# A hybrid attention layer on one core: low parts of the weights kept in DRAM, and half of the attention's transfers issued by GpSimd

## The chip, the cores and the metric

The kernel runs on one core of a Trainium2 chip. The metric is the time of one execution on the device in microseconds, measured over whole executions; the profile is one execution of its own, and its span goes from the first instruction to the last.

The core's engines run side by side, each through its own list of instructions, in order: TensorE (PE in the profile; PEld its weight loads), VectorE (DVE), ScalarE (ACT), GpSimd (POOL) and SyncE (SP), which here only issues transfers. An instruction waits for semaphores; while it waits, everything behind it on its engine waits too.

## The reference

One decoder layer over 2048 tokens of width 1024 in fp32. A single projection feeds three mixers: A, attention over the 256 best keys of an indexer; B, differential attention of two softmax maps; C, three dilated windows. Then the output projection, a norm, a gated feed-forward block and a second norm:

```python
def reference(x, w_in, w_o, lam, subln_g, ln1_g, ln1_b, w_gate, w_up, w_down, ln2_g, ln2_b):
    for l in range(DEPTH):
        lambda_init = 0.8 - 0.6 * math.exp(-0.3 * l)
        mix = hybrid_mixer(x, w_in[l], w_o[l], lam[l], subln_g[l], lambda_init)
        x = layer_norm(DEEPNORM_ALPHA * x + mix, ln1_g[l], ln1_b[l])
        f = (jax.nn.silu(x @ w_gate[l]) * (x @ w_up[l])) @ w_down[l]
        x = layer_norm(DEEPNORM_ALPHA * x + f, ln2_g[l], ln2_b[l])
    return x
```

## The kernel before

**Three products for one.** Every fp32 operand of the large products is split: its high part is the value rounded to the fp32r type, its low part is value minus high part, also fp32r. A product is then three matmuls: high by high, high by low, low by high (`mm3`, L1224 to L1230: L1227, L1228 and L1229 are these three; the low part of the weights enters in L1229).

**The order in time.** Until about 1169 us the kernel projects the input, ranks the keys for A and runs C together with A and B of the first 512 tokens. From there on two programs are woven together (`weave`, L751): the *trunk*, which takes the tokens in four groups g = 0 to 3 of 512, and the *attention* A and B of groups 1 to 3, which runs ahead of the trunk. For each group the trunk has a `head` (L1242: transpose the mixed rows, output projection `wo`, norm, transpose again) and a `body` (L1319: gate `fg`, up `fu` and down `fd` products in six stages `HV` of 4 or 3 chunks of 128 hidden columns). A planner in `weave` hands out the two programs by estimated costs, and a scheduler beneath it sets the final order of each engine's list at build time; at run time the lists are fixed.

**The weights' stream.** A `Stream` (L484) brings the weights of the trunk as tiles: w_o, gate and up tiles of 128x1024, down tiles of 128x512 or 128x384. `read` loads a raw tile (`fr` in the profile, two buffers), `divide` splits it by `split` (L149): ACT rounds the high part (L151), then POOL subtracts for the low part (L152; DVE instead for the tiles numbered 0, 2 and 4 of each stage, `HURRY`), both into one tile `f` with two buffers. `take` splits one tile ahead of the one that PE works on and reads two more. Each group streams and splits all weights anew. A raw buffer is free again when both the rounding and the subtraction are done, so the next load into it waits for POOL or DVE.

**The transfers.** `load` and `store` (L143 to L147) are both issued by SP: the raw weights, all loads of A and B (keys `ak`, `bk`, queries `aq`, `bq`, values `va`, `vb`, selection `se`), their results to DRAM (`mixd<-oa`, `mixd<-ob`), the mixed rows for the heads (`mx`, L1235: 128x1024 in two buffers `mx`), the residual rows `r` and the output. POOL issues only the joined results of C. On SP and on POOL alike a transfer may also wait for the one issued eight before it on the same engine, since each engine has eight semaphores for them.

Of the kernel before, what the change touches and what calls it, by code (L numbers as in the profile page):

```python
# [21 lines left out]
P = 128  # L22
# [28 lines left out]
F_RAWS = 2  # L51
NORMS = (0, 2)
# [6 lines left out]
RL = 3  # L59
MX_BUFS = 2  # L60
# [31 lines left out]
def tile_hybrid_layer(  # L92
# [391 lines left out]
    class Stream:  # L484
# [3 lines left out]
        def __init__(self, pool_, specs, raws, bufs, name, hurried=()):  # L488
            self.pool, self.specs, self.raws, self.bufs, self.name = pool_, specs, raws, bufs, name
            self.raw, self.tiles, self.pos, self.hurried = [], [], 0, hurried  # L490

        def read(self, upto):
            while len(self.raw) < min(upto, len(self.specs)):
                src = self.specs[len(self.raw)]
                n = src.shape[1]
                t = self.pool.tile([P, 1024], F32, name=f"{self.name}r{len(self.raw)}", tag="raw", bufs=self.raws)[:, :n]
                load(t, src)
                self.raw.append((t, n))

        def divide(self, upto):  # L500
            while len(self.tiles) < min(upto, len(self.specs)):
                i = len(self.tiles)
                self.read(i + 1)
                r, n = self.raw[i]
# [32 lines left out]
    def project(pt, w_, tl):  # L537
        wv = w_.rearrange("p a (k n) -> p a k n", k=KC)
        for k in range(KC):
            PE.matmul(pt, wv[:, 0, k], tl[0][:, k], start=(k == 0), stop=False)  # L540
            PE.matmul(pt, wv[:, 0, k], tl[1][:, k], start=False, stop=False)  # L541
            PE.matmul(pt, wv[:, 1, k], tl[0][:, k], start=False, stop=(k == KC - 1))  # L542
# [37 lines left out]
    def natural(kns, n, tl, name, tiles):  # L580
# [196 lines left out]
    def a_block(tp, g, qb, tab, ak, va):  # L777
# [6 lines left out]
        for r in (0, 64):  # L784
            load(q[r:r + 64].rearrange("p a h t -> p (a h) t").bitcast(F32), qad.rearrange("a (h r) t -> r (a h) t", r=64)[:, :, cols])
        if qb >= 2:
            se = tp.tile([P, wg_], BF16, name=f"se{qb}", tag="se")
            load(se[:, :w], seld[qb][:, :w])
# [29 lines left out]
        store(mixd[cols, 0:256], oa)  # L818
# [46 lines left out]
    def b_head(tp, g, h, tab):  # L865
# [6 lines left out]
        for m in range(2):  # L872
            k = tp.tile([P, wg_], F32R, name=f"bk{h}{m}_{g}", tag="bk", bufs=BK_BUFS[g])
            for r in range(0, P, 32):
                load(k[r:r + 32].bitcast(F32), kbd[r // 32 % 2, (2 * h + m) * 32:(2 * h + m + 1) * 32, 0:wg_])
            ks.append(k)
        for r in range(0, P, 32):
            load(q[r:r + 32].bitcast(F32), qbd[r // 64, h * 64:h * 64 + 64].rearrange("(m r) t -> r m t", m=2)[:, :, cols])
        vb = tp.tile([P, 4 * g + 4, P], F32R, name=f"vb{h}_{g}", tag="vb")
        load(vb.bitcast(F32), vbd[h].rearrange("(b p) d -> p b d", p=P)[:, 0:4 * g + 4, :])  # L880
# [36 lines left out]
        store(mixd.rearrange("(b p) d -> p b d", p=P)[:, 4 * g:4 * g + 4, 256 + h * 64:320 + h * 64], ob)  # L917

    def attention(g):
# [25 lines left out]
        load(ak.bitcast(F32), kad[:, 0:wg_])  # L945
        va = tp.tile([P, 4 * g + 4, P], F32R, name=f"va{g}")
        load(va.bitcast(F32), vad.rearrange("(b p) d -> p b d", p=P)[:, 0:4 * g + 4])
# [264 lines left out]
    f_specs, hurried = [], set()  # L1212
    for g in range(4):
        if g < 3:
            f_specs += [w_o[dc] for dc in range(8)]
        for f0, nf in HV:
            hurried.update(len(f_specs) + i for i in HURRY)
            for f in range(f0, f0 + nf):
                f_specs += ([w_gate[f]] if f > f0 or not f0 or g < EARLY else []) + [w_up[f]]
# [300 lines left out]
```

## Time and profile before

| | us |
|---|---|
| median of 3 runs | 3438.15 (3437.69 to 3444.48) |
| the profiled execution | 3439.7 |
| its span | 3437.9 |
| PE busy in the span | 3140.8 (91%) |
| POOL busy | 985.1 (29%) |
| DMA, mean over the span | 434.76 MB, 126 GB/s |

The table's lower part is from the profile's first part and from its line on DMA. A busy PE is not PE at its peak, because the ends of matmuls are modelled; what is sure is where PE stood still, and at what granted clock it ran. Those two are read from the waits and from tables of stretches.

### The profile page before, as it was taken

The page shows a single profiled execution, that of the slowest core. Times are in us where ns is not written, and L with a number is a line of the kernel's source. Part 1 is how long each engine was busy: PE and PEld are TensorE (multiplying, and loading weights), DVE is VectorE, ACT ScalarE, POOL GpSimd, SP SyncE. Part 2 cuts the span into 40 slices and gives each one's busy share as a digit, 9 for nine tenths or more (in the row PEclk, how much of TensorE's full clock was granted, in tenths as well). Part 3 has the DMA queues.
Part 4 walks back from the last instruction along what each step waited for, and adds up shares of the span by engine and source line. Part 5 has one row for each costly group of instructions (what it writes and reads, how often), then busy time and mean ns, then how long its engine had stood idle before and what let it go on. Part 6 is the DMA issues. An engine that isn't in the chain of part 4 may idle for free.

```text
span 3437.9 us, 45436 instructions
## 1 busy us (share of the span) xinstructions
PE 3140.8 (91%) x15994; PEld 2596.8 (76%) x15994; DVE 2076.5 (60%) x5353; ACT 1648.1 (48%) x2767; POOL 985.1 (29%) x587
## 2 busy tenths in 40 slices
PE   8898889858978799989998999999899999999997
PEld 7776667758878678877876788777678788778885
DVE  4879699546788576645458655465855555352224
ACT  3756646436756355545443545354454444232222
POOL 3221323014232222232223223321423232343332
PEclk9999999979999799999999999999999999999999
DMA  7464655588776633242245332423434232333322
GB/s 219 159 182 134 198 169 175 168 185 201 183 149 150 192 93 107 83 116 71 67 120 156 93 105 85 128 63 82 138 97 118 79 117 71 137 103 95 98 87 85
DMA packets 261206, 434.76 MB, mean 126 GB/s; under 512 B 49648, under 2 KB 149488, under 8 KB 256624
## 3 DMA queue, kind: packets, MB, share of 16 engines
q1 hardware_dynamic: 257776, 427.65, 43.8%
q0 software_dynamic: 1120, 3.67, 0.5%
q8 instruction: 126, 2.06, 0.3%
q14 instruction: 104, 0.85, 0.1%
q10 hardware_dynamic: 2080, 0.52, 0.1%
HBM read 331.65 MB, written 100.11 MB: 126 GB/s over the span
## 4 chain that ended last, share of the span: by engine, by line
PE 53%; DVE 6%; DMA 3%; issue 2%; ACT 2%; POOL 1%; SPq 0%; DVEq 0%; ACTq 0%; POOLq 0%
PE fg L1229 4%; PE fu L1229 4%; PE fu L1227 4%; PE fg L1227 4%; PE fu L1228 4%; PE fg L1228 4%; PE fd L1229 4%; PE fd L1227 4%; PE fd L1228 4%; PE wo L1227 1%; PE wo L1229 1%; PE wo L1228 1%; PE a_0o L854 1%; PE a_2o L854 1%; PE a_0t L845 1%
## 5 line engine op out<-in xcount | busy, mean ns | idle before, releaser
L152 POOL TENSOR_TENSOR f<-fr,f 128x1024 fp32r<-128x1024 f32 (+2 forms) x320 | 567.9, 1776 | 1438.5 <-ACT f L151 1389.9
L151 ACT CAST f<-fr 128x1024 fp32r<-128x1024 f32 (+2 forms) x392 | 321.4, 820 | 499.6 <-PE fd L1229 168.8
L1229 PE MATMUL fd<-h,f 128*128 128x512 f32 x704 | 282.1, 401 | 9.9 <-POOL f L152 9.9
L1227 PE MATMUL fd<-h,f 128*128 128x512 f32 x704 | 284.7, 405 | 4.1 <-ACT f L151 4.1
L1227 PE MATMUL fg<-xt,f 128*128 128x512 f32 x704 | 281.8, 400 | 0.8 <-DVE b_13m L895 0.3
L1227 PE MATMUL fu<-xt,f 128*128 128x512 f32 x704 | 281.2, 399 | 1.5 <-ACT f L151 1.5
L1229 PE MATMUL fg<-xt,f 128*128 128x512 f32 x704 | 278.8, 396 | 4.0 <-DVE f L152 2.9
L1228 PE MATMUL fd<-h,f 128*128 128x512 f32 x704 | 281.4, 400 | 0.0
L1229 PE MATMUL fu<-xt,f 128*128 128x512 f32 x704 | 278.4, 395 | 2.2 <-DVE f L152 1.2
L1228 PE MATMUL fg<-xt,f 128*128 128x512 f32 x704 | 278.2, 395 | 0.0
L1228 PE MATMUL fu<-xt,f 128*128 128x512 f32 x704 | 277.6, 394 | 0.0
L540 PE MATMUL pj<-xt,w 128*128 128x512 f32 x544 | 219.0, 403 | 26.6 <-DVE st L563 9.9
L542 PE MATMUL pj<-xt,w 128*128 128x512 f32 x544 | 216.7, 399 | 1.4 <-POOL w L152 1.4
L541 PE MATMUL pj<-xt,w 128*128 128x512 f32 x544 | 216.8, 399 | 0.7 <-POOL xt L152 0.7
L1355 DVE TENSOR_TENSOR fu<-sg,fu 128x512 f32<-128x512 f32 x88 | 61.1, 694 | 247.1 <-PE fu L1229 205.2
L1023 ACT ACTIVATE c<-c,ob 128x256 f32<-128x256 f32 (+1 forms) x384 | 156.5, 457 | 102.6 <-DVE ob L1017 101.7
L1371 DVE TENSOR_TENSOR rT<-rT,fd 128x512 f32<-128x512 f32 x160 | 109.4, 685 | 145.7 <-PE fd L1229 144.8
L1229 PEld LDWEIGHTS fd<-h,f 128*128 128x128 f32 x704 | 134.9, 192 | 42.3 <-POOL f L152 15.9
L152 POOL TENSOR_TENSOR w<-wr,w 128x1024 fp32r<-128x1024 f32 (+2 forms) x42 | 99.7, 2378 | 221.8 <-ACT w L151 186.3
L1227 PEld LDWEIGHTS fd<-h,f 128*128 128x128 f32 x704 | 134.9, 192 | 31.9 <-ACT f L151 6.8
L1229 PEld LDWEIGHTS fg<-xt,f 128*128 128x128 f32 x704 | 132.6, 188 | 32.8 <-DVE f L152 4.0
L1229 PEld LDWEIGHTS fu<-xt,f 128*128 128x128 f32 x704 | 132.5, 188 | 31.7 <-DVE f L152 3.0
(813 smaller groups left out, 8061.2 us busy)
## 6 DMA issues: line engine op xcount, KB each, us to landing
fr<-in_w_gate_dram SPq DMA_DIRECT2D x88, 512.0 KB
fr<-in_w_up_dram SPq DMA_DIRECT2D x88, 512.0 KB
fr<-in_w_down_dram SPq DMA_DIRECT2D x128, 256.0 KB
wr<-in_w_in_dram SPq DMA_DIRECT2D x42, 512.0 KB
fr<-in_w_o_dram SPq DMA_DIRECT2D x24, 512.0 KB
fr<-in_w_down_dram SPq DMA_DIRECT2D x64, 192.0 KB
ocd<-ob SPq DMA_DIRECT2D x16, 528.0 KB
ot<-ocd SPq DMA_DIRECT2D x32, 264.0 KB
```

The lines of the kernel that those rows point to most:

```text
L151: A.copy(hi, src)
L152: lo_eng.tensor_tensor(lo, src, hi.bitcast(F32), op=ALU.subtract)
L540: PE.matmul(pt, wv[:, 0, k], tl[0][:, k], start=(k == 0), stop=False)
L541: PE.matmul(pt, wv[:, 0, k], tl[1][:, k], start=False, stop=False)
L542: PE.matmul(pt, wv[:, 1, k], tl[0][:, k], start=False, stop=(k == KC - 1))
L854: PE.matmul(acc[:, :m], vfun(b), pt[:, i, c0:c0 + m], start=(b == 0 and i == 0), stop=(b == n - 1 and i == 1))
L1023: A.activation(nl, nl, AF.Exp, bias=ob[:, place(blk), 65:66], scale=-1.0)
L1227: PE.matmul(pt, wv[:, 0, k], hi[:, k], start=(k == 0), stop=False)
L1228: PE.matmul(pt, wv[:, 0, k], lo[:, k], start=False, stop=False)
L1229: PE.matmul(pt, wv[:, 1, k], hi[:, k], start=False, stop=(k == n - 1))
L1355: V.tensor_tensor(pt, sg, pt, op=ALU.mult)
L1371: V.tensor_tensor(d, d, pt, op=ALU.add)
```

## The change

**Low parts kept.** `Stream` gets a list of DRAM tensors, one for each weight tile (`lowd`). High and low part become two tiles, `f` with two buffers and `fl` with three. The first group still subtracts, and stores each low part to DRAM (100 stores, 37 MiB). In groups 1 to 3 SP loads the low parts (292 loads, 107 MiB), and their subtractions are gone: 238 on POOL and 54 on DVE. The stream of the last head's w_o (`g`) and that of the projection split as before.

**Transfers by POOL.** `fetch` issues from POOL where g is 2 or 3, from SP otherwise. By it go all loads and stores of A and B, the mixed rows and the residual rows: 172 transfers move from SP to POOL. The attention of group 2 begins while the trunk is still in group 0.

**Mixed rows in halves.** `read_mix` loads 128x512 into the four buffers `sg` that the gate's results use, in place of two buffers of its own.

```diff
+    def fetch(g, dst, src):
+        (G if g > 1 and OWN_QUEUE else SY).dma_start(out=dst, in_=src)
...
-        def __init__(self, pool_, specs, raws, bufs, name, hurried=()):
+        def __init__(self, pool_, specs, raws, bufs, name, hurried=(), kept=None, ahead=0):
...
                 load(t, src)
                 self.raw.append((t, n))
+                j = i - self.raws
+                if 0 <= j < len(self.tiles) and self.kept[j] is not None and id(self.kept[j]) not in self.stored:
+                    self.stored.add(id(self.kept[j]))
+                    store(self.kept[j], self.tiles[j][1][:, :self.raw[j][1]].bitcast(F32))
+
+        def low(self, upto):
+            while len(self.lows) < min(upto, len(self.specs)):
+                i = len(self.lows)
+                t = self.pool.tile([P, 1024], F32R, name=f"{self.name}l{i}", tag="wl", bufs=self.bufs + self.ahead)
+                there = self.kept[i] is not None and id(self.kept[i]) in self.stored
+                if there:
+                    load(t[:, :self.specs[i].shape[1]].bitcast(F32), self.kept[i])
+                self.lows.append((t, there))
...
-                t = self.pool.tile([P, 2, 1024], F32R, name=f"{self.name}{i}", tag="w", bufs=self.bufs)
-                split(t[:, 0, :n], t[:, 1, :n], r, V if i in self.hurried else G)
-                self.tiles.append(t)
+                hi = self.pool.tile([P, 1024], F32R, name=f"{self.name}{i}", tag="w", bufs=self.bufs)
+                lo, there = self.lows[i]
+                A.copy(hi[:, :n], r)
+                if not there:
+                    (V if i in self.hurried else G).tensor_tensor(lo[:, :n], r, hi[:, :n].bitcast(F32), op=ALU.subtract)
+                self.tiles.append((hi, lo))
...
             self.divide(i + min(n + 2, self.bufs))
+            self.low(i + self.bufs + self.ahead)
             self.read(len(self.tiles) + self.raws)
...
             for r in range(0, P, 32):
-                load(k[r:r + 32].bitcast(F32), kbd[r // 32 % 2, (2 * h + m) * 32:(2 * h + m + 1) * 32, 0:wg_])
+                fetch(g, k[r:r + 32].bitcast(F32), kbd[r // 32 % 2, (2 * h + m) * 32:(2 * h + m + 1) * 32, 0:wg_])
...
-    def read_mix(hp, g, t):
-        mx = hp.tile([P, D], F32, name=f"mx{g}{t}", tag="mx", bufs=MX_BUFS)
-        load(mx, mixd[rows(g, t), :])
+    def read_mix(hp, g, i):
+        mx = hp.tile([P, 512], F32, name=f"mx{g}{i}", tag="sg", bufs=RL)
+        fetch(g, mx, mixd[rows(g, i // 2), i % 2 * 512:i % 2 * 512 + 512])
...
-    fs = Stream(fp, f_specs, F_RAWS, F_BUFS, "f", hurried)
+    fs = Stream(fp, f_specs, F_RAWS, F_BUFS, "f", hurried, [lowd[key] for key in f_keys], 1)
```

**Where instructions stand now.** The scheduler orders all engines anew, so that small shifts are found everywhere. At three places the lists differ in kind. In them L152 is `fetch` in the changed kernel, L144 and L147 are `load` and `store`, L532 is the subtraction.

SP's list in the body of group 1. Before, raw tiles and the attention's loads alternate:

```order
L144 DMA fr_20030<-in_w_gate_dram 128x1024
L144 DMA fr_20069<-in_w_up_dram 128x1024
L144 DMA bq_2_20289<-qbd 32x2x512 x3
L144 DMA bk_2_21187<-kbd 32x1536
L144 DMA fr_20134<-in_w_down_dram 128x512
L144 DMA bk_2_21187<-kbd 32x1536 x3
```

After, nothing but a low part and a raw tile in turn:

```order
L144 DMA fl_20302<-lowu_13507 128x1024
L144 DMA fr_20304<-in_w_gate_dram 128x1024
L144 DMA fl_20355<-lowg_13508 128x1024
L144 DMA fr_20357<-in_w_up_dram 128x1024
L144 DMA fl_20399<-lowu_13509 128x1024
L144 DMA fr_20401<-in_w_gate_dram 128x1024
```

The attention's loads have left SP here, and each low part stands one place ahead of a raw tile.

POOL's list in group 0, stage 16 (down tiles of 128x384, numbered dc 0 to 7), where B of group 2 begins. Before, POOL makes the table of distances and then only low parts:

```order
L152 TENSOR_TENSOR f_18258<-fr_18132,f_18258 128x384
L773 IOTA tab_18360 128x1536
L775 AFFINE_SELECT tab_18360<-tab_18360 128x128
L152 TENSOR_TENSOR f_18326<-fr_18197,f_18326 128x384
L152 TENSOR_TENSOR f_18346<-fr_18261,f_18346 128x384
L152 TENSOR_TENSOR f_18391<-fr_18329,f_18391 128x384
```

After, the results of A's last two blocks and the first head's loads stand between them:

```order
L532 TENSOR_TENSOR fl_18500<-fr_18434,f_18563 128x384
L800 IOTA tab_18671 128x1536
L152 DMA bk_2_18677<-kbd 32x1536
L152 DMA mixd<-oa_17760 128x256
L532 TENSOR_TENSOR fl_18566<-fr_18501,f_18633 128x384
L152 DMA mixd<-oa_17774 128x256
L532 TENSOR_TENSOR fl_18636<-fr_18567,f_18655 128x384
L802 AFFINE_SELECT tab_18671<-tab_18671 128x128
L152 DMA bk_2_18677<-kbd 32x1536 x3
L152 DMA bk_2_18682<-kbd 32x1536 x4
L152 DMA bq_2_18676<-qbd 32x2x512 x4
L152 DMA vb_2_18691<-vbd 128x12x128
```

Twelve transfers in a row stand behind the low part of dc 2 (`fl_18636`) and ahead of that of dc 3. On PE the head's first logits, which stood behind all of dc 3 and dc 4, now stand behind their first two matmuls alone.

The start of A of group 3, in the body of group 1. Before, on SP, the loads stand between raw tiles:

```order
L147 DMA mixd<-ob_2_21203 128x4x64
L144 DMA fr_22053<-in_w_up_dram 128x1024
L144 DMA ak_22073<-kad 128x2048
L144 DMA va_22075<-vad 128x16x128
L144 DMA aq_22077<-qad 64x8x128 x2
L144 DMA se_22080<-sel_102 128x1664
L144 DMA aq_22088<-qad 64x8x128 x2
L144 DMA fr_22116<-in_w_down_dram 128x512
```

After, on POOL, which has no low parts to make here:

```order
L152 DMA mixd<-ob_2_21602 128x4x64
L152 DMA ak_22493<-kad 128x2048
L152 DMA va_22495<-vad 128x16x128
L152 DMA aq_22497<-qad 64x8x128 x2
L152 DMA se_22500<-sel_102 128x1664
L800 IOTA bi_22502 128x1664
L152 DMA aq_22508<-qad 64x8x128
L802 AFFINE_SELECT bi_22502<-bi_22502 128x128
```

The loads follow the last result of group 2's B at once, with no raw tile between.

## Rows read from the trace of the kernel before

**Rows 1.** The page's first part: busy time, share of the span, instructions.

```profile
span 3437.9 us, 45436 instructions
...
PE 3140.8 (91%) x15994; PEld 2596.8 (76%) x15994; DVE 2076.5 (60%) x5353; ACT 1648.1 (48%) x2767; POOL 985.1 (29%) x587
```

**Rows 2.** Table of stretches: ends, length, busy us by engine, granted clock, DMA share, GB/s.

```profile
1273.70:1803.80 530.10, 511.40 (x2535) 413.44 (x2535) 290.13 (x727) 264.55 (x392) 142.62 (x88) 0.97 0.32 92
...
1900.40:2426.20 525.80, 508.95 (x2519) 409.64 (x2518) 286.41 (x678) 249.39 (x344) 150.03 (x88) 0.99 0.34 96
```

**Rows 3.** PE's waits, 1803.8 to 3100 us: line, waited for, us in total, times, longest.

```profile
PE fd L1229 <- POOL f L152: 6.9, 4, 2.3
...
PE mt L1264 <- DMA mx<-mixd: 5.0, 3, 2.8
PE b_0l L826 <- DMA bq<-qbd: 4.9, 1, 4.9
...
PE a_0l L826 <- DMA aq<-qad: 2.6, 1, 2.6
...
PE a_0l L826 <- DVE a_0m L828: 2.2, 1, 2.2
```

**Rows 4.** Table of further stretches, columns as in rows 2.

```profile
790.00:1130.00 340.00, 288.44 (x2258) 272.93 (x2257) 265.88 (x1232) 212.06 (x515) 116.94 (x117) 0.93 0.73 164
...
1719.00:1741.00 22.00, 15.72 (x48) 10.40 (x47) 6.99 (x17) 5.30 (x8) 5.34 (x6) 0.78 0.80 198
...
2180.00:2210.00 30.00, 25.25 (x99) 19.43 (x98) 12.43 (x39) 8.67 (x11) 12.62 (x6) 0.89 0.58 149
2404.00:2414.00 10.00, 5.87 (x12) 3.34 (x12) 4.71 (x14) 2.69 (x4) 1.97 (x2) 0.66 0.73 185
...
2680.00:2710.00 30.00, 25.44 (x104) 20.17 (x103) 16.28 (x32) 9.08 (x12) 11.96 (x6) 0.89 0.30 97
```

**Rows 5.** SP's waits over the span, columns as in rows 3.

```profile
SPq L144 <- POOL f L152: 1268.8, 302, 23.4
```

**Rows 6.** Groups of instructions: shapes, count, busy us, mean ns, idle before, releasers.

```profile
L1371 DVE TENSOR_TENSOR rT<-rT,fd 128x512 f32<-128x512 f32 x160 | 109.4, 685 | 145.7 <-PE fd L1229 144.8
...
L152 POOL TENSOR_TENSOR f<-fr,f 128x1024 fp32r<-128x1024 f32 (+2 forms) x320 | 567.9, 1776 | 1438.5 <-ACT f L151 1389.9 <-PE b_1l L826 24.4 <-PE wo L1229 7.1
```

**Rows 7.** Tile mixd: transfers by line and issuer, ns of an issue (min/median/max); POOL's landing.

```profile
L147 SPq DMA_DIRECT2D mixd<-oa x16: 326/336/432, 767.8 to 2393.3; - x16
...
L1111 POOL DMA_DIRECT2D mixd<-ot x14: 926/927/1062, 802.3 to 1127.5; - x14
...
DMA to landing us min/median/max: 3.2/6.6/10.7
```

**Rows 8.** SP in order of time: start us, us, line, transfer, count.

```profile
1719.83 2.75 SPq L144 DMA_DIRECT2D bk<-kbd  x6
1722.69 2.12 SPq L144 DMA_DIRECT2D bq<-qbd  x4
```

**Rows 9.** POOL in order of time, the low part of dc 3.

```profile
1720.02 1.02 POOL L152 TENSOR_TENSOR f<-fr,f 128x384 fp32r<-128x384 f32 x1 [0.59 <-ACT f L151]
```

**Rows 10.** PE in order of time; in brackets idle before and releaser.

```profile
1724.95 0.40 PE L1228 MATMUL fd<-h,f 128*128 128x512 f32 x1
...
1725.88 0.39 PE L1229 MATMUL fd<-h,f 128*128 128x512 f32 x1
1730.37 0.73 PE L826 MATMUL b_0l<-bk,bq 128*128 128x512 f32 x2 [4.10 <-DMA bq<-qbd]
```

**Rows 11.** SP in order of time, where A of group 3 begins.

```profile
2172.79 5.14 SPq L144 DMA_DIRECT2D aq<-qad  x2
```

**Rows 12.** SP in order of time, where B of group 3 begins.

```profile
2396.98 3.24 SPq L144 DMA_DIRECT2D bq<-qbd  x4
```

**Rows 13.** SP in order of time, a raw tile of 128x384 in group 3.

```profile
3360.23 0.33 SPq L144 DMA_DIRECT2D fr<-in_w_down_dram  x1
```

**Rows 14.** ACT in order of time, the rounding of that tile.

```profile
3362.71 0.52 ACT L151 CAST f<-fr 128x384 fp32r<-128x384 f32 x1 [1.95 <-DMA fr<-in_w_down_dram]
```

More of the change, by code (lines that the diff above doesn't have):

```diff
@@ L484, in tile_hybrid_layer @@
     class Stream:
-        def __init__(self, pool_, specs, raws, bufs, name, hurried=()):
+        def __init__(self, pool_, specs, raws, bufs, name, hurried=(), kept=None, ahead=0):
             self.pool, self.specs, self.raws, self.bufs, self.name = pool_, specs, raws, bufs, name
-            self.raw, self.tiles, self.pos, self.hurried = [], [], 0, hurried
+            self.raw, self.lows, self.tiles, self.pos, self.hurried = [], [], [], 0, hurried
+            self.kept, self.ahead, self.stored = kept or [None] * len(specs), ahead, set()
         def read(self, upto):
             while len(self.raw) < min(upto, len(self.specs)):
-                src = self.specs[len(self.raw)]
+                i = len(self.raw)
+                src = self.specs[i]
                 n = src.shape[1]
-                t = self.pool.tile([P, 1024], F32, name=f"{self.name}r{len(self.raw)}", tag="raw", bufs=self.raws)[:, :n]
+                t = self.pool.tile([P, 1024], F32, name=f"{self.name}r{i}", tag="raw", bufs=self.raws)[:, :n]
                 load(t, src)
                 self.raw.append((t, n))
+                j = i - self.raws
[10 more added lines that the diff above has]
+                self.lows.append((t, there))
         def divide(self, upto):
@@ L817, in a_block @@
         yield 0.0, 1.0
-        store(mixd[cols, 0:256], oa)
+        fetch(g, mixd[cols, 0:256], oa)
     def logits(qs, k, bias, nl, w, ms, name):
@@ L916, in b_head @@
         yield 0.0, 5.0
-        store(mixd.rearrange("(b p) d -> p b d", p=P)[:, 4 * g:4 * g + 4, 256 + h * 64:320 + h * 64], ob)
+        fetch(g, mixd.rearrange("(b p) d -> p b d", p=P)[:, 4 * g:4 * g + 4, 256 + h * 64:320 + h * 64], ob)
     def attention(g):
@@ L1211, in tile_hybrid_layer, with want_f @@
     HV = [(0, 4), (4, 4), (8, 4), (12, 4), (16, 3), (19, 3)]
-    f_specs, hurried = [], set()
+    f_specs, f_keys, hurried = [], [], set()
+    def want_f(w, name, *at):
+        f_specs.append(w)
+        f_keys.append((name, *at))
     for g in range(4):
         if g < 3:
-            f_specs += [w_o[dc] for dc in range(8)]
+            for dc in range(8):
+                want_f(w_o[dc], "o", dc)
         for f0, nf in HV:
@@ L1218, in tile_hybrid_layer @@
             for f in range(f0, f0 + nf):
-                f_specs += ([w_gate[f]] if f > f0 or not f0 or g < EARLY else []) + [w_up[f]]
+                if f > f0 or not f0 or g < EARLY:
+                    want_f(w_gate[f], "g", f)
+                want_f(w_up[f], "u", f)
             if f0 + nf < FC and g >= EARLY:
-                f_specs.append(w_gate[f0 + nf])
-            f_specs += [w_down[dc][:, f0 * P:(f0 + nf) * P] for dc in range(8)]
+                want_f(w_gate[f0 + nf], "g", f0 + nf)
+            for dc in range(8):
+                want_f(w_down[dc][:, f0 * P:(f0 + nf) * P], "d", dc, f0)
+    lowd = {}
+    for w, key in zip(f_specs, f_keys):
+        if key not in lowd:
+            lowd[key] = dram.tile([P, w.shape[1]], F32, name="low" + "_".join(map(str, key)))
     def mm3(pt, w_, n, hi, lo):
-        wv = w_[:, :, :n * P].rearrange("p a (k c) -> p a k c", c=P)
+        wh, wl = (w[:, :n * P].rearrange("p (k c) -> p k c", c=P) for w in w_)
         for k in range(n):
-            PE.matmul(pt, wv[:, 0, k], hi[:, k], start=(k == 0), stop=False)
-            PE.matmul(pt, wv[:, 0, k], lo[:, k], start=False, stop=False)
-            PE.matmul(pt, wv[:, 1, k], hi[:, k], start=False, stop=(k == n - 1))
+            PE.matmul(pt, wh[:, k], hi[:, k], start=(k == 0), stop=False)
+            PE.matmul(pt, wh[:, k], lo[:, k], start=False, stop=False)
+            PE.matmul(pt, wl[:, k], hi[:, k], start=False, stop=(k == n - 1))
             yield 0.64, 0.0
@@ L1361, in body @@
                 if f0 + nf == FC and g < 2 and ready[0] > g and g + 1 not in early_mix:
-                    early_mix[g + 1] = [read_mix(fp, g + 1, i) for i in range(MX_BUFS)]
+                    early_mix[g + 1] = [read_mix(fp, g + 1, i) for i in range(RL)]
                 w_ = fs.take(1)[0]
```

47 lines of the change are left out of this document (24 added, 23 removed).

## Prediction

> **What bounds the kernel now.** I read the share of busy time first. PE is busy 91% of the span, and POOL, from which the change takes most work, 29% [rows 1]; so it can only pay where PE stands still or runs at a lower clock. The table of stretches says how little that is: the body of the first group fills 511.40 of 530.10 us with matmuls, at a granted clock of 0.97, that of the second 508.95 of 525.80 at 0.99 [rows 2]. Some 18 us a body is all that any edit can win there. PE's waits from 1803.8 to 3100 us, the part without subtractions after the change, name what is late there [rows 3]: low parts from POOL, `f`, 6.9 us in 4 waits; mixed rows `mx` 5.0; the queries `bq` of one B, 4.9; the queries `aq` of one A, 2.6; and 2.2 behind them for DVE. A wait costs more than its length: four stretches around such waits were granted 0.78, 0.89, 0.66 and 0.89 of the clock [rows 4], so between the two levels of 2.4 and 1.2 GHz, after PE had stood. One minus the clock, times the length, gives 4.8, 3.3, 3.4 and 3.3 us; this is a ceiling, since a low clock during idle time costs nothing.
>
> SP's list shows the second fact. It stood 1268.8 us in 302 waits for POOL's subtractions [rows 5], since a raw buffer is free only after them, and whatever attention load stands behind such a raw tile is late with it.
>
> The profiled execution took 3439.7 us with a span of 3437.9, the median is 3438.15. The sum is a difference, so I subtract it from the median; the profiled run lies 0.05% above that.
>
> **Low parts kept.** It removes 238 subtractions of POOL at a mean of 1.776 us [rows 6], 238 x 1.776 = 423 us of POOL, and 54 of DVE. Nearly all lies beside matmuls. On the path are the waits for it: 6.9 us for POOL's low parts [rows 3], about 2 for DVE's, and the stretch at 2680 with 3.3 us of clock. Of these 12 I take 10, since a raw tile rounded late still holds PE: **-10**, bounds -12 and -3. DVE, relieved of 54 subtractions, gives -1 (0 to -3).
>
> It adds 100 stores and 292 loads on SP. A raw tile costs SP 0.33 us an issue [rows 13], so 100 x 0.33 = 33 us in group 0 and 96 us later, spread between tiles, where SP stands waiting anyway [rows 5]. The cover is SP's waits; without it the stores alone could cost 33 us. A store stands behind nothing but the next raw load, so +1 (0 to +3). Bytes: 144 MiB, 151 MB, in some 2150 us add 70 GB/s to 92 to 96 [rows 2]; stretches at 198 GB/s occur [rows 4], so bandwidth has room. What counts is when a low part lands. A raw tile of 128x384 was issued at 3360.23 and rounded from 3362.71 [rows 13, 14], so it landed within 2.48 us. Four matmuls take 0.93 us, from 1724.95 to 1725.88 [rows 10], 0.23 each; a down tile of 384 has 9, 2.1 us. With three buffers the load starts when the tile three places earlier is done, and has two tiles, 4.2 us. 2.48 fits: 0.
>
> **Transfers by POOL.** The price of an issue: POOL's 14 stores of C took 926, 927 and 1062 ns (least, median, most), SP's stores into the same tensor 326, 336 and 432 [rows 7]. POOL's were the more divided (128 rows of 8 pieces of 64 numbers, against 32 or 64 rows in a load of keys or queries), so I take 0.93 for all 172, though SP's own issues differ by shape: `bk` 2.75/6 = 0.46, `bq` 2.12/4 = 0.53 [rows 8]. Growth as on SP would make it 0.93 x 0.46/0.336 = 1.27 us, the upper end. 172 x 0.93 = 160 us of POOL, covered by the 423 it loses, except in three places where they stand in a row and PE waits for the last.
>
> *B of group 2, in group 0.* On SP the last `bq` was issued by 1722.69 + 2.12 = 1724.81 [rows 8], and PE went on at 1730.37 after 4.10 us of idle [rows 10]: landing 5.56. In POOL's order seven `bk` and four `bq` follow the low part of dc 2, which ends some 0.6 us ahead of that of dc 3 (1720.02, after 0.59 of idle [rows 9]), so at 1719.4; with the table's step 1719.7. Eleven issues make 1719.7 + 11 x 0.93 = 1729.9, and landing as before 1735.5, 5.1 later. With the shortest landing in the table of `mixd`, 3.2 [rows 7], it is 2.7 later. Also, 16 of the 18 matmuls of dc 3 and dc 4 stood ahead of the logits and now stand behind: 16 x 0.23 = 3.7 us, part of which fills DVE's later waits. Ends +3 and +9; I take **+6**. The low part of dc 3 waits too, 12 x 0.93 = 11.2 us, but no longer than these logits hold PE.
>
> *A of group 2, in group 0.* Eight transfers stand between low parts of another stage: 7.4 us, against two down tiles of 512 that are split ahead, 2 x 12 x 0.23 = 5.5; and SP's queue no longer delays A there: **+1** (-2 to +5). Four stores of results, for which POOL waits on DVE, hold low parts behind them: +1 (0 to +3).
>
> *A of group 3.* SP needed 5.14 us for two `aq` [rows 11], against a clean price of 0.4 to 0.5 each: it stood behind a raw tile. POOL has nothing to subtract there and issues them at once. Of 2.6 us for `aq`, 2.2 behind it [rows 3] and 3.3 of clock [rows 4], I take 7: **-7** (-8 to 0).
>
> A rule on whether a queue of its own helps: the Trainium skill, page "DMA: Bandwidth & Descriptors", section "Issuing engines are not separate DMA queues", says that several issuing engines save only the time the sequencer needs to start transfers. By that rule the -7 is not there. Rows 5 are against it: SP's time here is standing behind waits, which is no time to start a transfer.
>
> *B of group 3.* Twelve issues cost POOL 11.2 us; SP took 3.24 for the four `bq` [rows 12], and about as much for the keys ahead of them. POOL may begin earlier, since no raw tile stands in its list: **+2** (-8 to +6). The mixed rows come in smaller pieces, through POOL and in buffers that the gate's results share: 0 (-5 to +3).
>
> **Sum:** -10 - 1 + 1 + 6 + 1 + 1 - 7 + 2 = -7; the anew made order may shift 3 us either way. 3438.15 - 7 = **3431**, own range 3420 to 3442 from the middle of the bounds.
>
> **Rivals.** *Issues on POOL dearer (slower).* Thirty-one issues stand exposed: 11 for B of group 2, 8 for its A, 12 for B of group 3. The time is 3431 + 31 x (p - 0.93), with p the mean issue: equal to before at 1.16 us, slower by 0.2% at 1.38. The mechanism: POOL's issue is held while DVE works. DVE's commonest instruction in the trunk takes 0.685 us [rows 6]; one such hold an issue gives p = 1.6, so 3452. Against it: all 14 known issues stayed below 1.07 us [rows 7], in a stretch where DVE was busy 265.88 of 340 us [rows 4], more than anywhere in the trunk (290.13 of 530.10 [rows 2]). For it: loads are not stores, and nothing shows POOL issuing one.
>
> The Trainium skill speaks for this rival: "SBUF — State Buffer", section "Who interferes with whom", has GpSimd locked out, its writing of descriptors included, while DVE runs copies and tensor-scalar instructions in a two-port mode. By its rule a hold each would give the 3452 above; the 14 short issues don't show it.
>
> *Full gain.* Loads leave without SP's waits and early enough that B's twelve are hidden: `bq` 4.9, its clock 3.4 and `mx` 5.0 go too, and +2 and +6 don't come: 3431 - 13.3 - 8 = 3410. Against it: the two-deep rows of issues.
>
> *A queue of its own saves nothing* (the sequencer's time alone counts): A of group 3 stays as it is, 3431 + 7 = 3438.
>
> *Low parts land late (slower).* If 2.48 us become 5.6 as around B's loads, the missing 1.4 us beyond 4.2 falls on two tiles in flight, 0.7 each, over the 48 down tiles of 384 in groups 1 to 3: +34, 3465. Decides from 4.2 us. Against: 2.48 with the stream at 96 GB/s.
>
> **How the numbers follow.** Forecast 0.45 (3431); dear issues 0.23 (3452); full gain 0.16 (3410); no saving 0.10 (3438); late low parts 0.06 (3465). A measurement of this kernel tells 0.2% from no change, so 3431.3 and 3445.0 are the bounds. Half of the forecast's share lies below 3431.3, the rest within; full gain is faster, no saving the same, the two slower rivals slower but for a small part: faster 0.40, same 0.32, slower 0.28. Range: from below 3410 to the upper side of dear issues, 3404 to 3457; late low parts and the ends of the rivals are left out.
>
> **What would show it.** POOL's transfers in the changed kernel: a mean of 0.9 to 1.0 us by issue is the forecast, above 1.38 the first rival. PE's waits: `b_0l` for `bq` near 1735 at 6 to 13 us of idle; near 2180 no wait of `a_0l` for `aq`; no wait of `fd` or `fg` for POOL after 1804; waits of `fd` for a DMA of `fl`, repeated at each down tile, would be the late low parts. POOL busy (transfers aren't counted) about 985 - 423 = 562 us, DMA 435 + 151 = 586 MB. The forecast is wrong if PE's idle time in groups 1 to 3 doesn't fall, or if it falls and group 0 gives back more than 8 us.

## The result, and the profile after

The changed kernel took 3486.62 us (the median of 6 runs), the kernel before 3437.92 beside it: a ratio of 1.0136, 95% interval 1.0124 to 1.0148. It is 49 us slower where 7 us faster was forecast, and outside the range of 3404 to 3457. The profiled execution has a span of 3484.5 us, so it is 46.6 us longer than that of before [rows 1]. The page's first part, busy time with its share of the span:

```profile
span 3484.5 us, 45726 instructions
...
PE 3156.9 (91%) x15994; PEld 2606.9 (75%) x15994; DVE 2003.8 (58%) x5299; ACT 1650.0 (47%) x2767; POOL 657.8 (19%) x521
```

POOL's busy time here holds its transfers too, which the prediction's 562 us left out. The subtractions fell as worked out, from 320 to 82, and the bytes rose to 585.8 MB as forecast. PE is busy 16 us longer with the same number of matmuls, at a lower granted clock (0.951 over the span, before 0.960), and some 30 us of the 46.6 are new idle time. Where they lie is read from a table of stretches, with the columns of [rows 2]; it is cut at the first instruction of each stage on PE: head of group 0 (first `mt`), its body (first `fg`), head of group 1 (first `ft` of group 0, the transposes that end a body), and so on. From group 2 on the order on PE is another: the head of group 3 begins (first `mt`) while group 2 still has down products to do, and its first gate and up products come ahead of the first `ft` of group 2. So body 2 is cut at the first `mt` of group 3, and "head 3" is the mixture from there to the first `ft` of group 2.

```profile
0.00:1181.50 1181.50, 992.04 (x5575) 858.47 (x5575) 874.01 (x2537) 662.41 (x1355) 310.87 (x215) 0.92 0.63 173
...
1823.80:1929.70 105.90, 83.71 (x435) 67.96 (x434) 80.26 (x211) 44.92 (x71) 15.97 (x14) 0.92 0.59 187
1929.70:2447.60 517.90, 504.66 (x2501) 406.37 (x2502) 245.13 (x618) 242.41 (x336) 60.61 (x74) 0.98 0.54 162
2447.60:2577.60 130.00, 103.81 (x494) 79.23 (x492) 100.06 (x278) 57.07 (x83) 24.73 (x26) 0.84 0.50 154
2577.60:2970.60 393.00, 383.37 (x1841) 317.33 (x1842) 188.19 (x452) 182.69 (x238) 19.53 (x34) 0.99 0.55 171
2970.60:3084.60 114.00, 106.77 (x491) 85.22 (x492) 38.26 (x80) 38.80 (x58) 22.84 (x15) 0.96 0.43 143
```

The same cuts in the profiles of all kernels of this study give this table (us; each from one profiled execution, so a few us of any entry are the execution's own):

| kernel | projection | head 0 | body 0 | head 1 | body 1 | head 2 | body 2 | head 3 | body 3 | span |
|---|---|---|---|---|---|---|---|---|---|---|
| before | 1168.8 | 104.9 | 530.2 | 96.6 | 525.8 | 106.6 | 396.0 | 106.7 | 402.4 | 3437.9 |
| changed | 1181.5 | 103.5 | 538.8 | 105.9 | 517.8 | 130.1 | 393.0 | 114.0 | 400.0 | 3484.5 |
| e1 tiles split | 1166.5 | 104.7 | 531.5 | 103.4 | 524.4 | 110.1 | 394.6 | 102.2 | 403.9 | 3441.2 |
| e2 + POOL's queue | 1167.9 | 104.7 | 533.9 | 113.7 | 535.9 | 112.9 | 395.7 | 108.7 | 403.0 | 3476.3 |
| e3 + halves | 1173.5 | 103.9 | 531.0 | 98.4 | 526.0 | 107.2 | 394.4 | 104.2 | 401.5 | 3440.1 |
| e4 + halves, kept | 1175.4 | 104.9 | 538.6 | 95.6 | 524.7 | 99.5 | 390.1 | 103.8 | 397.5 | 3430.1 |
| e5 e4, A by POOL | 1177.5 | 104.6 | 539.2 | 99.1 | 514.4 | 103.6 | 391.7 | 105.3 | 398.0 | 3433.5 |
| e6 e4, B by POOL | 1168.5 | 105.1 | 539.1 | 105.1 | 522.1 | 110.5 | 391.2 | 103.3 | 398.0 | 3442.8 |
| e7 e4, heads by POOL | 1174.7 | 104.0 | 538.4 | 98.9 | 522.0 | 100.4 | 392.5 | 109.0 | 402.9 | 3442.8 |
| e8 changed, head 1 too | 1173.2 | 103.8 | 536.7 | 99.8 | 519.1 | 128.1 | 394.7 | 114.8 | 396.9 | 3467.0 |
| f1 changed, B of 3 by SP | 1174.2 | 102.6 | 536.9 | 106.8 | 520.2 | 100.4 | 390.9 | 112.2 | 400.1 | 3444.4 |
| f2 changed, B of 2 by SP | 1170.3 | 102.6 | 537.1 | 101.4 | 513.1 | 129.2 | 393.3 | 113.5 | 398.3 | 3458.8 |
| f3 e4, A of 3 by POOL | 1169.8 | 103.8 | 536.0 | 96.8 | 515.9 | 97.1 | 389.5 | 103.1 | 400.5 | 3412.7 |
| f4 e5, stores by POOL | 1177.0 | 105.5 | 536.2 | 96.2 | 516.3 | 103.2 | 390.7 | 105.5 | 397.3 | 3428.0 |

Changed against before: the bodies of groups 1 to 3 are 13.4 us shorter, where the prediction's terms for them add up to -18 (-10, -1 and -7). Body 0 is 8.6 longer, the heads of groups 1, 2 and 3 are 9.3, 23.5 and 7.3 longer, the projection 12.7. The heads were priced at nothing but B of group 3, +2. PE's idle time in groups 1 to 3, whose fall was to be the sign of the forecast, rose by 17 us.

**Head 1.** The lists of the changed kernel there: POOL first, then SP (start us, us, transfer, count; in brackets the idle time before and what ended it).

```profile
1821.27 1.98 POOL L152 DMA_DIRECT2D bk<-kbd  x4
1825.35 2.13 POOL L152 DMA_DIRECT2D bq<-qbd  x4 [2.09 <-PE b_1l L853]
1829.54 0.51 POOL L152 DMA_DIRECT2D bk<-kbd  x1 [2.06 <-DMA bk<-kbd]
```

```profile
1835.24 1.36 SPq L152 DMA_DIRECT2D mx<-mixd  x2
...
1837.13 0.90 SPq L152 DMA_DIRECT2D mx<-mixd  x2
1840.06 4.22 SPq L152 DMA_DIRECT2D r<-in_x_dram  x2
```

And who waits, on PE and on ACT:

```profile
1832.27 2.09 PE L1368 MATMUL ft<-ident,rT 128*128 128x128 f32 x12 [4.43 <-ACT o L165]
...
1845.94 1.09 PE L1304 MATMUL mt<-ident,mx 128*128 128x128 f32 x4 [7.19 <-DMA mx<-mixd]
```

```profile
1830.68 1.04 ACT L530 CAST f<-fr 128x1024 fp32r<-128x1024 f32 x1 [4.43 <-DMA fr<-in_w_o_dram]
```

When POOL has no low part left to make, its list runs free: four `bk`, four `bq` and four more `bk` of B of group 2 leave from 1821.27 on, the first of them 14 us ahead of the fifth half of the mixed rows (the first four halves had been read early; the others wait for their buffers). They are under way together with w_o and then with the mixed rows. The second raw tile of w_o, issued at 1821.36, lets ACT go on at 1830.68, 9.3 us later (in e4 6.0, from 1816.42 to 1822.45); it holds up ACT for 4.43 us and so the transposes `ft`. The fifth half, issued at 1835.24, lets PE go on at 1845.94, 10.7 us later (in e4 5.3, from 1826.16 to 1831.46), after 7.19 us of idle. With everything on SP (e4) three of B's loads stand right behind the mixed rows and the other nine later still. The first 31 us of this head in the two kernels, changed and e4, columns as in [rows 2]:

```profile
1823.80:1855.00 31.20, 16.86 (x101) 14.48 (x100) 16.80 (x39) 12.65 (x21) 4.13 (x8) 0.78 0.92 267
```

```profile
1818.90:1850.00 31.10, 25.11 (x159) 20.53 (x158) 27.44 (x57) 16.31 (x27) 4.38 (x2) 1.00 0.81 255
```

The DMA engines are busy 0.92 of the time against 0.81, and PE 16.86 us against 25.11, with a granted clock of 0.78 (a mix of the two levels of 1.2 and 2.4 GHz, after PE had stood) against 1.00.

**Head 2.** This stretch in the kernel before, columns as in [rows 2]; that of the changed kernel is the one from 2447.60 in the table of stretches above:

```profile
2426.20:2532.80 106.60, 89.52 (x469) 72.14 (x468) 84.47 (x216) 46.45 (x70) 37.34 (x13) 0.92 0.45 137
```

So of the 23.5 us 9.1 are idle time of PE (26.2 against 17.1) and 14.3 busy time: 25 more matmuls of B stand in it (494 against 469), which the bodies beside it have lost, at a granted clock of 0.84 against 0.92. PE and DVE of the changed kernel where B of group 3 begins, and the line on the landing of its queries:

```profile
2453.84 0.71 PE L853 MATMUL b_0l<-bk,bq 128*128 128x512 f32 x2
2464.26 0.79 PE L853 MATMUL b_0l<-bk,bq 128*128 128x512 f32 x1 [9.72 <-DVE b_13m L855]
```

```profile
2459.79 1.54 DVE L1466 TENSOR_SCALAR o<-o,mvb,lrb 128x1024 f32<-128x1024 f32 x2
2461.24 2.36 DVE L1468 TENSOR_TENSOR o<-o,gb 128x1024 f32<-128x1024 f32 x2
2463.51 0.69 DVE L855 CUSTOM_DVE_ANT_0 b_13p<-b_0l,tab 128x512 f32<-128x512 f32 x1
```

```profile
L152 POOL DMA_DIRECT2D bq<-qbd x4: 533/540/546, 2421.9 to 2425.2; - x4
...
DMA to landing us min/median/max: 9.8/10.0/10.3
```

The last `bq` was issued at 2425.2 and landed within 10.3 us, by 2436. PE came to the first logits at 2453.84, since in its list they stand behind the last down products, the transposes `ft` and the first `mt`; in the kernel before they stand 61 matmuls ahead of the first `ft`, here 40 behind it. On DVE the maximum of these logits stands behind the norm of two blocks of group 1, so PE idles 9.72 us more. Neither is a late transfer: it is the order of the lists, which the scheduler made anew around POOL's loads.

**Where B of group 2 begins.** This is the place that the prediction priced most carefully:

```profile
1734.15 1.00 POOL L532 TENSOR_TENSOR fl<-fr,f 128x384 fp32r<-128x384 f32 x1 [1.21 <-ACT f L530]
...
1735.35 3.41 POOL L152 DMA_DIRECT2D bk<-kbd  x7
...
1741.59 0.53 POOL L152 DMA_DIRECT2D bq<-qbd  x1 [0.55 <-DMA bk<-kbd]
```

```profile
1747.48 1.19 PE L853 MATMUL b_0l<-bk,bq 128*128 128x512 f32 x2 [8.42 <-DMA bq<-qbd]
```

### The profile page after: what moved, and what is told of

The parts are those of the page before. It is cut to its first block, busy times and chain, and to the rows that moved or that the text cites. A ratio compares the mean times of both kernels' runs of the same rounds, so it can differ in the third digit from the quotient of the medians.

```text
span 3484.5 us, 45726 instructions
## 1 busy us (share of the span) xinstructions
PE 3156.9 (91%) x15994; PEld 2606.9 (75%) x15994; DVE 2003.8 (58%) x5299; ACT 1650.0 (47%) x2767; POOL 657.8 (19%) x521
## 4 chain that ended last, share of the span: by engine, by line
PE 52%; DMA 6%; DVE 4%; ACT 1%; issue 1%; POOL 1%; SPq 0%; DVEq 0%; ACTq 0%; POOLq 0%
PE fg L1267 4%; PE fg L1269 4%; PE fg L1268 4%; PE fu L1269 4%; PE fu L1267 4%; PE fu L1268 4%; PE fd L1267 4%; PE fd L1269 4%; PE fd L1268 4%; PE wo L1269 1%; PE wo L1268 1%; PE wo L1267 1%; PE a_0o L881 1%; PE a_2o L881 1%; DMA se<-sel 1%
## 5 line engine op out<-in xcount | busy, mean ns | idle before, releaser
L1267 PE MATMUL fd<-h,f 128*128 128x512 f32 x704 | 283.4, 403 | 10.7 <-ACT f L530 10.7
L1269 PE MATMUL fd<-h,fl 128*128 128x512 f32 x704 | 280.2, 399 | 5.6 <-DMA fl<-lowd 4.0
L1267 PE MATMUL fg<-xt,f 128*128 128x512 f32 x704 | 283.6, 403 | 1.8 <-ACT f L530 0.8
L1269 PE MATMUL fu<-xt,fl 128*128 128x512 f32 x704 | 278.5, 396 | 3.1 <-DMA fl<-lowu 1.7
L1267 PE MATMUL fu<-xt,f 128*128 128x512 f32 x704 | 281.0, 399 | 0.0
L1269 PE MATMUL fg<-xt,fl 128*128 128x512 f32 x704 | 279.8, 397 | 1.1 <-DVE fl L532 1.0
L1268 PE MATMUL fd<-h,f 128*128 128x512 f32 x704 | 279.1, 397 | 0.0
L1268 PE MATMUL fg<-xt,f 128*128 128x512 f32 x704 | 277.9, 395 | 0.0
L1268 PE MATMUL fu<-xt,f 128*128 128x512 f32 x704 | 276.8, 393 | 0.0
L567 PE MATMUL pj<-xt,w 128*128 128x512 f32 x544 | 221.5, 408 | 28.5 <-DVE st L590 8.8
L568 PE MATMUL pj<-xt,w 128*128 128x512 f32 x544 | 219.3, 403 | 0.7 <-POOL xt L157 0.7
L569 PE MATMUL pj<-xt,wl 128*128 128x512 f32 x544 | 218.6, 402 | 1.4 <-POOL wl L532 1.4
L532 POOL TENSOR_TENSOR fl<-fr,f 128x1024 fp32r<-128x1024 f32 (+2 forms) x82 | 142.9, 1744 | 400.7 <-ACT f L530 385.6
L1050 ACT ACTIVATE c<-c,ob 128x256 f32<-128x256 f32 (+1 forms) x384 | 156.6, 456 | 104.1 <-DVE ob L1044 103.4
L1267 PEld LDWEIGHTS fd<-h,f 128*128 128x128 f32 x704 | 134.1, 191 | 38.6 <-ACT f L530 13.7
```

The source lines that it names most:

```text
L532: (V if i in self.hurried else G).tensor_tensor(lo[:, :n], r, hi[:, :n].bitcast(F32), op=ALU.subtract)
L567: PE.matmul(pt, hi[:, k], tl[0][:, k], start=(k == 0), stop=False)
L568: PE.matmul(pt, hi[:, k], tl[1][:, k], start=False, stop=False)
L569: PE.matmul(pt, lo[:, k], tl[0][:, k], start=False, stop=(k == KC - 1))
L1050: A.activation(nl, nl, AF.Exp, bias=ob[:, place(blk), 65:66], scale=-1.0)
L1267: PE.matmul(pt, wh[:, k], hi[:, k], start=(k == 0), stop=False)
```

## The experiments

Every experiment is the changed kernel with switches, so all have the weight tiles split into `f` and `fl`. The comparisons are ratios to the kernel before, run beside it on the same chip. So ratios are compared and not medians. An expected time in us can miss by a few us for that reason alone: the kernel before took 3437.92 us beside the changed kernel and 3431 to 3433 beside all others.

**The four ingredients.** e1: nothing kept, mixed rows whole, all transfers by SP.

```diff
-OWN_QUEUE = True
-RL = 4
+OWN_QUEUE = False
+RL = 3
...
-    fs = Stream(fp, f_specs, F_RAWS, F_BUFS, "f", hurried, [lowd[key] for key in f_keys], 1)
+    fs = Stream(fp, f_specs, F_RAWS, F_BUFS, "f", hurried, None, 0)
...
+        mx = hp.tile([P, D], F32, name=f"mx{g}{i}", tag="mx", bufs=2)
+        fetch(g, mx, mixd[rows(g, i), :])
```

> Only the split of each weight tile into two tiles, high and low, is left of the change; SP issues everything, mixed rows come whole, nothing is kept in DRAM. Theory (the anew made order costs, whatever part of the change causes it): the projection, in which nothing else was changed, ends some 12 us later as in the changed kernel, and the time is 3445 to 3455. Rival (the cost is in the transfers by POOL, in the halves or in the kept low parts): 3438, the same as before within 5 us.

3443.44 us, ratio 1.0043 (1.0029 to 1.0057). Both were wrong in part: the projection took 1166.5 us, not 12 more, and the time rose by 0.4%; in the profile heads 1 and 2 are 10 us longer. Splitting a tile in two, which changes no transfer and no instruction's work, costs 0.4%, some 11 to 15 us. What is left for it is the order of the lists (at 1501 of PE's 15994 places stands a matmul of another tile) and when the two halves come free; which of them isn't told apart.

e2: e1 with POOL's queue.

```diff
-OWN_QUEUE = False
+OWN_QUEUE = True
```

> POOL issues the transfers of A, B and the heads for groups 2 and 3; low parts are made anew in every group, mixed rows come whole. Theory (POOL's queue moves B of group 3 into the head of group 2, where DVE has the norm to do): the head of group 2 takes over 120 us against 107, the time is 20 to 30 us above that of the kernel with split tiles alone. Rival (the queue is harmless, the kept low parts or the halves cost): within 5 us of it.

3479.15 us, ratio 1.0147 (1.0121 to 1.0173): 1.0% or 36 us above e1. The loss of the changed kernel is there without a single kept low part. The place was missed: head 1 (+10), body 1 (+11.5) and head 3 (+6.5) carry it here, head 2 only 3. In this kernel B of group 3 begins inside body 1, and PE waits there 9.5 us for its queries.

e3: e1 with the mixed rows in halves, as the changed kernel has them.

```diff
-RL = 3
+RL = 4
...
+        mx = hp.tile([P, 512], F32, name=f"mx{g}{i}", tag="sg", bufs=RL)
```

> Only the mixed rows come in halves, into the gate's buffers (with split tiles); SP issues all, nothing is kept. Theory (halves start late, since they wait for the gate's results): PE waits 7 us for them in the head of group 1 and the time is 5 to 15 us above that of the kernel with split tiles alone. Rival (halves are free): within 4 us of it.

3441.56 us, ratio 1.0024 (1.0011 to 1.0037), no slower than e1: the rival holds, halves on SP are free within the intervals.

e4: the changed kernel with all transfers on SP.

```diff
-OWN_QUEUE = True
+OWN_QUEUE = False
```

> The changed kernel with all transfers on SP: low parts kept, mixed rows in halves. Theory (POOL's queue is what costs, the kept low parts gain 10 us in the bodies of groups 1 to 3): 3430 to 3450, the head of group 2 back at 107 us. Rival (the traffic of the low parts costs): 3475 or more, with long waits of PE for the low parts.

3431.56 us, ratio 1.0002 (0.9988 to 1.0015); head 2 takes 99.5 us. The theory holds: against e3 the kept low parts gain 0.2% (10 us between the medians; the two intervals just overlap), in the profiles some 20 us in groups 1 to 3 less 7.6 in body 0. Nothing but the issuer and the order that follows from it separates e4 from the changed kernel, so POOL's issuing costs 1.3%, some 46 us.

**Which of POOL's transfers.** `fetch` gets a fourth argument, "A", "B" or "H" (mixed and residual rows), and POOL issues one kind only:

```diff
-    def fetch(g, dst, src):
-        (G if g > 1 and OWN_QUEUE else SY).dma_start(out=dst, in_=src)
+    def fetch(g, dst, src, part):
+        (G if g > 1 and part in PARTS else SY).dma_start(out=dst, in_=src)
```

e5, `PARTS = "A"`:

> The changed kernel, but POOL issues only A's transfers of groups 2 and 3 (keys, queries, values, selections, results); B's loads and the heads' rows are SP's. Theory (what costs is B's loads overtaking the rows that the heads need, once they stand in another list): about the time of the changed kernel with all on SP, 3432, within 8 us. Rival (whatever POOL issues lands late or costs at each place): a third of the loss, 3442 to 3450.

3422.84 us, ratio 0.9971 (0.9959 to 0.9984). That is 1 us below the theory's range, and the rival falls: POOL as issuer is no cost here but a gain, and it is in body 1, 514.4 us against 524.7.

e6, `PARTS = "B"`:

> POOL issues only B's loads and results of groups 2 and 3. Theory: most of the loss is here, 3455 to 3480, and the head of group 1 takes 105 us against 96 with all on SP, PE waiting 5 us or more there for the mixed rows. Rival (each part costs alike): 3442 to 3450.

3447.41 us, ratio 1.0046 (1.0029 to 1.0063). The place is right, the total is not: head 1 takes 105.1 us, with PE's wait for mixed rows (waits on PE in head 1: us in total, times, longest):

```profile
PE mt L1310 <- DMA mx<-mixd: 6.3, 1, 6.3
```

But 0.44% above e4, 15 us, is less than I expected, and the figure lies in the rival's range.

e7, `PARTS = "H"`:

> POOL issues only the mixed rows and residual rows of the heads of groups 2 and 3. Theory: the heads' rows now are free of SP's list, but B's loads stay with SP, so nothing overtakes: 3425 to 3440. Rival (each part costs alike): 3442 to 3450, in the heads of groups 2 and 3.

3441.00 us, ratio 1.0019 (1.0008 to 1.0030), just outside the theory's range and 0.17% above e4; in its profile head 3 is 5 us longer, and body 3 too. The heads' rows by POOL are no gain. By the ratios A gives -0.31%, B +0.44% and H +0.17% over e4, together +0.30%, but all three at once give +1.34%: most of the loss comes only when the three are issued by POOL together. That it is their order within POOL's list is the nearest reading, and is shown at single places alone (head 1 by e8 and f2, head 2 by f1, A of group 3 by f2).

e8: all three, and the rows of head 1 too (`g > 0` for "H").

> The changed kernel with the rows of the head of group 1 on POOL as well, so that they stand in one list with B's loads, most of these behind them. Theory (order between the lists): the head of group 1 is back at 96 to 99 us from 106, PE's wait there for mixed rows under 2 us, the time 3472 to 3480. Rival (POOL's transfers land late in themselves): the head of group 1 stays at 105 us or gets longer, 3485 or more.

3474.19 us, ratio 1.0128 (1.0106 to 1.0149). Head 1 falls from 105.9 to 99.8 us, and mixed rows are no longer among PE's seven largest waits there (6.1 us in two waits of `ft` for ACT lead them); the rival falls. In one list the mixed rows stand ahead of eight of the twelve loads of B. The 6 us don't show in the total, though, whose interval overlaps that of the changed kernel (1.0124 to 1.0148).

**The places.** f1: the changed kernel with the loads and results of B of group 3 on SP; f2: those of B of group 2.

```diff
+        (G if g > 1 and (part, g) != ("B", 3) else SY).dma_start(out=dst, in_=src)
```

> The changed kernel, but the loads and results of B of group 3 are SP's again. Its first logits then stand in PE's list 68 instructions ahead of the first transpose ft of group 1, in the changed kernel 10 behind it. Theory (PE's list, made anew around POOL's loads, puts B of group 3 into the head of group 2): the head of group 2 takes 100 to 106 us against 130, the time is 3455 to 3465. Rival (the head of group 2 is long because its mixed rows come by POOL): it stays at 120 us or more, 3480.

3448.56 us, ratio 1.0048 (1.0034 to 1.0062); head 2 takes 100.4 us against 130.1, with A and the mixed rows still on POOL. The theory holds: the time lies 6 us below the expected range, but as a gain over the changed kernel by the ratios, 0.9% or 30 us, it lies at the upper end of the expected 22 to 32. The list of PE in this kernel has the first logits 68 matmuls ahead of `ft` (in the changed kernel they stand 40 matmuls behind it, not 10).

> The changed kernel, but the loads and results of B of group 2 are SP's again, those of group 3 remain with POOL. Theory (B's loads of group 2 overtake the rows that the head of group 1 needs): the head of group 1 takes 96 to 99 us against 106, the head of group 2 stays at 125 to 130, the time is 3474 to 3480. Rival (the head of group 1 is long by clock or order alone): it stays at 105.

3459.32 us, ratio 1.0079 (1.0048 to 1.0111). Head 1 takes 101.4 us, between the two theories, and head 2 stays at 129.2. The total is 15 us below what I expected, some 7 of them by the kernel before, which was faster by as much. Body 1 is part of the rest, 513.1 us against 517.8 with the same matmuls: the results of group 2's B no longer stand in POOL's list, A's keys leave at 1867.6, and PE has no wait for `aq` there. In f1 and e8, where they do stand there, the keys leave at 2184.1 and 2175.8, and PE waits 4.5 and 4.6 us.

In all three kernels whose head 2 is at 128 to 130 us PE waits nearly 10 us at one logit; in e6, where B of group 3 also begins in the head but DVE has its maximum ahead of the norm, it doesn't, and head 2 takes 110.5. So beginning in the head costs some 11 us over the 99.5 of e4, and the maximum behind the norm most of the other 20, as far as kernels that differ at other places too can show it. PE's waits around head 2, of f2 and of e6:

```profile
PE b_0l L855 <- DVE b_13m L857: 13.2, 4, 9.9
```

```profile
PE b_0l L855 <- DVE b_13m L857: 0.8, 3, 0.5
```

**Towards a better kernel.** f3: e4 with only A of group 3 on POOL.

```diff
+        (G if g > 2 and part == "A" else SY).dma_start(out=dst, in_=src)
```

> POOL issues only A's transfers of group 3, where it has no low parts to make. Theory (the gain of 10 us by A's loads on POOL comes from A of group 3 alone, in the body of group 1, those of group 2 give nothing): the same as with A of both groups, 3423, within 5 us. Rival (A of group 2 gains too): 3430.

3423.30 us, ratio 0.9971 (0.9957 to 0.9986): as e5, so A of group 2 on POOL gives nothing. Why A of group 3 gains is seen from when its keys are issued, in f3 and in the changed kernel (POOL in order of time), and from PE's first logits of this A:

```profile
L154 POOL DMA_DIRECT2D ak<-kad x1: 592/592/592, 1864.6 to 1864.6; - x1
```

```profile
2192.24 0.76 POOL L152 DMA_DIRECT2D mixd<-ob  x1 [106.55 <-DVE ob L942]
2192.99 0.55 POOL L152 DMA_DIRECT2D ak<-kad  x1
2193.53 1.16 POOL L152 DMA_DIRECT2D va<-vad  x1
2194.68 1.38 POOL L152 DMA_DIRECT2D aq<-qad  x2
```

```profile
2183.62 0.63 PE L855 MATMUL a_0l<-ak,aq 128*128 128x512 f32 x2
```

```profile
2211.30 1.19 PE L853 MATMUL a_0l<-ak,aq 128*128 128x512 f32 x2 [5.33 <-DMA aq<-qad]
```

In e4, with SP as issuer, PE stands 10.9 us ahead of the logits of this A up to 2250 us, 1.3 of them for `aq` and 7.4 for DVE's maxima of logits; in f3, where the logits begin earlier and stand between other matmuls, it is 3.1, and none of it for `aq`. With nothing else in the way POOL issues the keys at 1864.6, over 300 us ahead of their use, and PE goes on at 2183.62 without a wait. In the changed kernel the same load stands behind `mixd<-ob`, for which POOL had waited 106.55 us on DVE; it leaves at 2192.99, and PE still waits 5.33 us for `aq`.

f4: e5, and POOL stores the low parts in group 0.

```diff
-                    store(self.kept[j], self.tiles[j][1][:, :self.raw[j][1]].bitcast(F32))
+                    G.dma_start(out=self.kept[j], in_=self.tiles[j][1][:, :self.raw[j][1]].bitcast(F32))
```

> POOL issues A's transfers of groups 2 and 3, and also stores the low parts in group 0, at the same places in the program where SP did. Theory (in group 0 the stores on SP, which wait for POOL, delay raw tiles, and this makes the body of group 0 some 8 us longer than before): the body of group 0 falls from 539 to 532 us, the time from 3423 to 3416. Rival (the stores' bytes cost, whoever issues them, or POOL's issues delay the low parts): 539 us or more, 3423 to 3430.

3423.64 us, ratio 0.9975 (0.9961 to 0.9990), the same as e5, and in the rival's range. Body 0 takes 536.2 us against 539.2, but 536.0 in f3, where SP stores: this settles nothing. Why body 0 grows by some 7 us once the low parts are stored (531.0 in e3, 538.6 in e4) stays open between the stores' places on SP, their bytes and the order.

## Why the prediction was wrong

**Right: the low parts kept.** The step said -10 and -1; e3 to e4 is 8 to 10 us in all, in the profiles some 20 us in groups 1 to 3 against 7.6 lost in body 0. If those 7.6 are the stores', their term, +1 with 0 to +3, was too small by some 6 us. Late low parts, the fifth case, didn't come: PE's waits for them in the changed kernel are a few us (the first of them below, columns as in [rows 3]).

```profile
PE fd L1269 <- DMA fl<-lowd: 4.0, 3, 2.0
```

**Wrong in size, and harmless: the price of an issue.** I took 0.93 us from the stores of C [rows 7] and made the slower rival from its growth. POOL's loads of 32 rows take 0.49 and 0.54 us, half of that (tile `bk` and tile `bq`: least, median, most in ns):

```profile
L152 POOL DMA_DIRECT2D bk<-kbd x64: 489/492/537, 1730.3 to 2794.6; - x64
```

```profile
L152 POOL DMA_DIRECT2D bq<-qbd x32: 533/541/548, 1738.8 to 2796.7; - x32
```

The more a transfer is divided, the longer POOL takes: `va`, 128 rows of 16 pieces, took 1.16 us at 2193.53. So B of group 2 came out much as worked out in its landing (5.4 us from the last issue at 1741.59 + 0.53 to PE at 1747.48, as 5.56 before), but only 1.4 us later, counted from the end of the low part of dc 2 (1735.15 here, 1719.4 before), and not 5.1; and body 0 as a whole is as long as in e4, where SP issues (538.8 and 538.6; PE's wait there 8.42 and 5.9 us), so the +6 doesn't show in the stage. By the prediction's own formula for 31 issues, 0.5 in place of 0.93 us would have made the kernel some 13 us faster than forecast. Dear issues, the rival with 0.23, named the right sign for a reason that didn't exist; had the time come out at its 3452, that would have been luck. The lock between DVE and GpSimd that the Trainium skill describes ("SBUF — State Buffer", section "Who interferes with whom") doesn't show either: no issue of `bk` took over 537 ns while DVE was busy 58% of the span.

**The step that failed: a list of its own, priced as a saving of waits alone.** Three terms hung on it. *A of group 3*, -7: the gain is there in f3 and e5 (9 and 10 us in body 1 against e4), where A is alone on POOL, but the changed kernel's list has the result of B ahead of A's keys, and the wait for DVE behind which SP's raw tiles had stood is now a wait behind which A's loads stand: PE's wait for `aq` went from 2.6 to 5.33 us, and is gone in f2, where that result left POOL's list. I had even quoted this row of the new order (`mixd<-ob` first) and read it as "issues them at once". *B of group 3*, +2: I counted the issues and not what the later loads would do to the lists; its first logits moved behind `ft` on PE and behind a norm on DVE. Head 2 grew by 23.5 us, and f1, with this B alone back on SP, is 0.9% or 30 us faster: this is the largest of the three misses. *Mixed rows*, 0 with -5 to +3: head 1 grew by 9.3 us, of which PE waited 7.19 for them. With POOL free of subtractions nothing held B's next loads back, and they overtook what the head needed; head 3, 7.3 longer, has waits for mixed rows as well (5.9 us against 2.1), but no experiment settles it. SP's waits [rows 5], which I took for pure loss, had also been what kept B's loads behind the rows that the head needed first.

The rule that I had set against it, from the Trainium skill's page "DMA: Bandwidth & Descriptors", section "Issuing engines are not separate DMA queues", says that transfers of all issuers run on the same 16 DMA engines and interleave there. Head 1 agrees: the DMA engines were 0.92 busy there, and the urgent transfers took longer than in e4 (9.3 and 10.7 us against 6.0 and 5.3). I used only its second half (a queue saves only the time of starting), which would have given 3438, and not its first, which names the harm.

**Wrong: the order made anew, within 3 us.** e1 changes nothing but the tiles and is 0.43% slower (interval 0.29% to 0.57%), 15 us. That the order of the whole program changes was known; its bound was guessed, and no row stood behind it.

**Open.** The projection, which the change doesn't touch, ran 12.7 us longer in the changed kernel's profile, with 9 us more of busy PE at a clock of 0.92 against 0.93, but between 1166.5 and 1177.5 in the others, with no relation to their edits (e5 and f3 differ in group 2 alone and lie 7.7 us apart). The execution alone can do as much: the profiled run of e5 was the slowest of its ten (3435.26 us, median 3422.84), that of f3 lay 8.8 us below its median. Whether the 12.7 us belong to the order or to the execution isn't settled.

## What to carry to other kernels

A queue's waits are also its priorities: before transfers go to an engine that will have nothing else to do, ask which of them will now leave early, and what urgent transfer is under way with them at that moment. Move one kind of transfer whose buffers are free long ahead and with no store in front of it (A's loads of group 3 alone: ratio 0.9971, interval 0.9957 to 0.9986, better than both kernels), and keep the loads that must come in turn in one list. Where a scheduler orders the engines, look up where the first consumer of each moved load now stands on PE and on DVE; a shift past a stage's end is a cost to be priced like a wait.

## What was not expected of the hardware

POOL starts a plain load of 32 rows in 0.49 to 0.54 us, not much above SP's 0.42 to 0.43 for the same, and its cost rises with the number of pieces (0.93 for the 1024 of C's stores, 1.04 to 1.16 for the 2048 of `va`). Its landing differs far more: the eight `bk` where B of group 2 begins took 3.0 to 6.5 us, eight others of the same size in the head of group 1, with the DMA engines 0.92 busy, 8.0 to 11.1. Over all `bk` by POOL in the changed kernel (least, median, most):

```profile
DMA to landing us min/median/max: 3.0/6.8/12.0
```
